# Attention weights of fifteen heads turned by a transposing DMA instead of TensorE

## The chip, the cores and the metric

The kernel runs on one core of one Trainium2 chip. The metric is the device time of one execution in microseconds; lower is better. Before the change the median of three runs is 2024.54 us (2023.59 to 2025.33).

## What is computed

One residual block on 512 rows of 2048 columns, in 32-bit floats: a norm, one input projection, sixteen attention heads of width 128 (eight with stick-breaking weights, eight with forgetting-gate softmax weights), a norm per head, an output projection, and a feed-forward part. The attention, cut to what matters here:

```python
# stick-breaking, per block of 128 queries:
z = einsum('bhqd,bhkd->bhqk', qb, kb) * scale
log_beta = log_sigmoid(z)
log_keep = where(causal, log_sigmoid(-z), 0.0)
rest = cumsum(log_keep, axis=3, reverse=True) - log_keep
a = where(causal, exp(log_beta + rest), 0.0)
o = einsum('bhqk,bhkd->bhqd', a, vb)
# forgetting: p = softmax(where(causal, z + c_q - c_k, -inf)); o = p @ vb
mixed = concat(head_rmsnorm(o_sb), head_rmsnorm(o_fox))
x = x + mixed @ w_out
```

## The kernel before

Every 32-bit matmul is done as three: each operand is split into a high part (ScalarE rounds it, `act.copy` to the type that TensorE reads in one pass) and a low part (VectorE subtracts the high part), and `mm3` (L74 to L78) multiplies high by high, high by low and low by high.

The attention stage runs in 17 periods, n = 0 to 16. In period n TensorE projects the q and k columns of head n (`project`: 16 row blocks of `w_in`, for q and then for k, three matmuls of 512 columns each, 96 in all, into the PSUM tile `accq`), computes the scores of head n - 1 (`scores`, into `s`), and forms the output of head n - 2 (`product`, into `o`) and the sums of squares of its norm (`norm_sums`, into `ssq`). Heads 0 to 7 in this order are forgetting heads, 8 to 15 stick-breaking heads. Period 16 has no projection left; it computes the last two heads' values (`accv`).

Between scores and product a head's weights pass through these steps. Stick-breaking: `start` and `soft` on ScalarE (absolute value, exponential, logarithm; L800, L803, L804), `maxed` on VectorE and a causal mask on GpSimd, `scan` (a running sum and a subtraction) on VectorE, `weights` on ScalarE (L817) and the mask again. Forgetting: `start` on VectorE with the mask, `maxed` on VectorE, `soft` on ScalarE, `scale` on VectorE. The result is `w`: 128 queries on the partitions by 1280 columns, the ten causal blocks of 128 by 128, in the places that `OFF_Q` gives.

The product needs the weights with the keys on the partitions. `turn` (L856 to L862) transposes the ten blocks on TensorE, against the identity, into the PSUM tile `pt`; `p_high` (ScalarE, L870) and `p_low` (VectorE, L873) split them into `ph` and `pl` in SBUF. `product` then multiplies, for each key block j, the value rows by the weights of queries j to 3 (512, 384, 256 and 128 columns, three matmuls each). `square`, `square_low`, `norm_sums`, `norm_1` (L914, L915) and `norm_2` (L920 to L923) make the head's norm; they reuse the buffers of `ph` and `pl`.

Beside that, ScalarE and VectorE split four 512 KB pieces of `w_in` per period (`wraw` to `wh` and `wl`, L168 and L175), scale and split q and k (`qf` to `uh` and `ul`), and form sums of `w_out` for the next stage (`WeightSums`: `tboth`, `thi`, `ws` or `mixed`), which SP stores to DRAM (`wraws`, `whigh`, `wsums`).

The order of every queue but GpSimd's comes from one list. `plan.at(t, f)` notes a job with a number, the place in the stage at which it should be issued; `Plan.run` sorts the jobs by it and calls them, and each engine, and SP with its DMAs, executes its own instructions in that order. The number sets nothing but the order. `TPER`, 27.05, is the number's step from period to period. Buffers and PSUM tiles have one copy each (`w`, `s`, `ph`, `pl`; `wraw` has three): a job waits until the last reader of what it overwrites is done.

Of the kernel before, what the change touches and what calls it, by code (L numbers as in the profile page):

```python
# [9 lines left out]
F32R = mybir.dt.float32r  # L10
AF = mybir.ActivationFunctionType
# [20 lines left out]
OFF_Q = [896, 1024, 512, 0]  # L32
# [4 lines left out]
def block_kernel(ctx, tc, x, g_attn, w_in, b_f, g_out_sb, g_out_fox, w_out, g_mlp, w_up, w_down, g_final, y):  # L37
# [667 lines left out]
    with tc.tile_pool(name="att", bufs=1, side="right", reuse_waits="tile") as at, \  # L705
# [69 lines left out]
        def causal(w, op, fill):  # L775

            for d, n in ((w[:, P:1280].rearrange("p (a b) -> p a b", b=384)[:, :, 256:], 3), (w[:, 896:1024], 1)):
                pool.affine_select(out=d, in_=d, compare_op=op, fill=fill, base=0,
                                   pattern=[[0, n], [-1, P]] if n > 1 else [[-1, P]], channel_multiplier=1)

        class Head:
# [4 lines left out]
            def scores(self):  # L786
                q, k = u_of[self.i, 0], u_of[self.i, 1]
                s = atp.tile([P, 1536], F32, tag="s", name="s")
                for i in (3, 2, 0, 1):
                    n = (i + 1) * P  # L790
                    qs = slice(i * P, (i + 1) * P)
                    mm3(s[:, OFF_Q[i]:OFF_Q[i] + n], q[0][:, qs], q[1][:, qs], k[0][:, :n], k[1][:, :n], i != 0, True)
                self.s = s[:, :1280]

            def plan_sb(self, plan, t):
                g = self.h

                def start():
                    self.w = wide("w")
                    act.activation(self.w, self.s, AF.Abs)  # L800

                def soft():
                    act.activation(self.w, self.w, AF.Exp, scale=-1.0)  # L803
                    act.activation(self.w, self.w, AF.Ln, bias=1.0)  # L804

                def maxed():
                    dve.scalar_tensor_tensor(self.w, self.s, 0.0, self.w, op0=ALU.max, op1=ALU.add)
                    causal(self.w, ALU.is_gt, 0.0)

                def scan():  # L810
                    for r in rows(self.w):

                        dve.tensor_tensor_scan(r[:, ::-1], r[:, ::-1], r[:, ::-1], 0.0, op0=ALU.add, op1=ALU.max)
                    dve.tensor_tensor(self.w, self.s, self.w, op=ALU.subtract)

                def weights():
                    act.activation(self.w, self.w, AF.Exp)  # L817
                    causal(self.w, ALU.is_gt, 0.0)

                for dt, f in ((8.45, start), (9.75, soft), (12.4, maxed), (15.2, scan), (20.1, weights)):  # L820
                    plan.at(t + dt, f)

            def plan_fox(self, plan, t):
# [28 lines left out]
                times = (6.5, 9.3, 11.0, 14.0) if self.i == 0 else (10.85, 14.6, 16.8, 20.1)  # L852
                for dt, f in zip((-4.0, *times), (load, start, maxed, soft, scale)):
                    plan.at(t + dt, f)
# [8 lines left out]

            def p_high(self):
                if self.i < 2 * NH - 1:
                    self.ph, self.pl = wide("ph", F32R), wide("pl", F32R)
                else:
                    both = at.tile([P, 2, 1280], F32R, tag="ws", name="p_last")
                    self.ph, self.pl = both[:, 0], both[:, 1]
                act.copy(self.ph, self.pt[:, :1280])  # L870
# [92 lines left out]
        def whole(m, t):  # L963
            w = WeightSums(m, (0, 1), lambda: mixed[:, :NH].rearrange("p (q a) n -> p q (a n)", a=2))
            loads, first, second = ((-15.0 if m > 1 else -13.5, 2.7), (21.5, 22.3, TPER + 3.3), (TPER + 1.75, TPER + 2.5, TPER + 6.7)) if m else \
                ((20.5, 20.6), (TPER + 1.75, TPER + 2.5, TPER + 4.5), (TPER + 10.0, TPER + 10.7, TPER + 7.0))
            for i in range(2):
                plan.at(t + loads[i], w.load, (i,))
            for i, at_ in enumerate((first, second)):
                for dt, f in zip(at_, (w.high, w.low, w.sum)):  # L970
                    plan.at(t + dt, f, i)
            third, fourth = (TPER + 9.2, TPER + 17.5) if m else (TPER + 7.2, 2 * TPER + 0.9)
            for dt, f in ((second[2] + 0.1, lambda: w.store(0, 2)), (third, lambda: w.sum(2)), (fourth, lambda: w.sum(3)),
                          (2 * TPER + 1.75, w.high_6), (2 * TPER + 2.5, w.low_6), (2 * TPER + 2.6, lambda: w.store(2, 4))):
                plan.at(t + dt, f)

        def half(m, d, n):
# [8 lines left out]
            jobs = [(17.6 if n == 8 else 8.3, load if n == 7 else w.load)]  # L986
            if d == 0:
                c, a = (23.2, (1.75, 2.4, 3.1, 3.8, 5.6, 6.4)) if n > 7 else (16.4, (5.5, 6.3, 7.0, 9.0, 12.0, 17.4))
                jobs += [(c, lambda: w.high(0)), (c + 0.7, lambda: w.low(0)), (c + 1.2, lambda: w.sum(0)), (c + 2.0 if n > 7 else TPER + 3.5, lambda: w.sum(1))]
                jobs += [(TPER + dt, f) for dt, f in zip(a, (lambda: w.high(1), lambda: w.low(1), lambda: w.sum(2), lambda: w.sum(3), w.high_6, w.low_6))]  # L990
                jobs += [(TPER + a[-1] + 0.1, w.store)]
            else:
                at_ = (23.7, 24.4, 25.1, TPER + 2.4) if n > 8 else [TPER + dt for dt in (2.4, 3.1, 6.4, 7.1)]
                jobs += [(dt, lambda j=j: w.sum(j)) for j, dt in enumerate(at_)] + [(at_[-1] + 0.1, w.store)]
# [19 lines left out]
        TRI, TPER = 0.681, 27.05  # L1014
# [4 lines left out]
        for n in range(2 * NH + 1):  # L1019
            t = TPER * n  # L1020
            i_s, i_o = n - 1, n - 2
            if n < 2 * NH:
                pieces = []
                for a, (which, hf) in enumerate(((0, 0), (0, 1), (1, 0), (1, 1))):
# [3 lines left out]
                    cast, low = ((-11.7, -6.9), (0.3, 5.4), (5.6, 10.9), (12.45, 13.95))[a]  # L1028
                    load = cast - 16 if n != 2 or a else -21.4
                    if n == 1:  # L1030
                        load = -23.0 if a == 0 else load
                        cast, low = ((-7.0, -5.0), (-3.0, -2.0), (2.9, 3.9), (8.5, 9.5))[a]
                    if n == 0:
                        cast, low, load = 16.3, 18.2, 0.3
                    pieces.append(q_piece(n, which, hf).plan(plan, t + load, t + cast, t + low))
                marks = [(0, 0, 1, 0.0), (0, 1, 6, 2.6), (0, 6, 8, 8.4), (1, 0, 8, 9.75), (2, 0, 8, 15.2), (3, 0, 4, 20.6), (3, 4, 8, 24.4)]
# [4 lines left out]
                for which, dt in ((0, {0: 19.0, 1: 25.85}.get(n, 21.4)), (1, TPER + 0.3)):  # L1041
                    plan.at(t + dt, scale_u, n, which)
                    plan.at(t + dt + (0.65 if (n, which) == (1, 0) else 0.75), high_u, n, which)
                    plan.at(t + dt + (1.35 if (n, which) == (1, 0) else 1.45), low_u, n, which)
            else:
                pieces = []
                for a in range(4):
# [3 lines left out]
                    cast, low = ((-11.7, -6.9), (0.3, 3.3), (9.0, 10.0), (13.0, 14.5))[a]  # L1051
                    pieces.append(w.plan(plan, t + cast - 16, t + cast, t + low))
                unit = 0
                for a in range(4):
                    for tt in range(TB):
                        dt = 1.45 * unit + (0 if unit < 2 else 1.95) + (0 if unit < 13 else 1.1)
# [4 lines left out]
            if 0 <= i_s < 2 * NH:  # L1061
                H = heads[i_s]
                ts = t + 6.45 if n < 2 * NH else t + 2.95
                plan.at(ts, H.scores)
                (H.plan_sb if H.h < NH else H.plan_fox)(plan, ts - 6.45)
                tp = t + (20.4 if n == 1 else 23.3) if n < 2 * NH else t + 2.9 + 1.95 + 1.45 * 11 - 0.05
                plan.at(tp, H.turn)
                plan.at(tp + 1.2, H.p_high)
                plan.at(tp + 2.5, H.p_low)
                if i_s % 2 == 0 and i_s < 2 * NH - 2:  # L1070
                    p_ = i_s // 2
                    plan.at(t - 12.0 if p_ else t + 3.0, load_v, p_)
                    plan.at(t + (5.4 if i_s >= NH else 16.5), high_v, p_)
                    plan.at(t + (6.3 if i_s >= NH else 23.65 if p_ else 17.0), low_v, p_)
            if 0 <= i_o < 2 * NH - 2:
                H = heads[i_o]
                plan.at(t + 0.68, H.product)
                plan.at(t + 2.7, H.square)
                plan.at(t + 4.6, H.square_low)
                plan.at(t + 6.0, H.norm_sums)  # L1080
                plan.at(t + 6.55, H.norm_1)
                plan.at(t + 7.95, H.norm_2)
# [981 lines left out]
```

## Time and profile before

| | |
|---|---|
| median of three runs | 2024.54 us |
| profiled execution: its own time | 2023.56 us |
| its span in the profile | 2021.8 us |
| granted TensorE clock | 0.999 of full speed |
| attention stage | about 168 to 583 us of the span |
| TensorE transposes of the weights | 160 (L861), ten for each of 16 heads |

In the views' lines stand: start and duration in us, engine, line of the kernel, operation, output and inputs by name (buffer numbers left out), shapes and count. An `[idle <-X]` at the end says how long the engine had been idle and who ended it. PE is TensorE's matmuls, PEld its weight loads, DVE VectorE, ACT ScalarE, POOL GpSimd, SP the engine that issues the DMAs. Matmuls overlap, so their cost is read from start to start, not from their duration. A line of the windows view gives a stretch, its length, each engine's busy time (and instructions), granted clock, DMA share and GB/s; one of the DMA view gives the count of transfers, the KB of each, and the median time from issue to landing; one of the waits view gives who waited for whom, us in total, how often, and the longest.

### The profile page before, as it was taken

The numbers are of one execution on the slowest core, as the hardware profiler recorded it, in microseconds if no ns is written. First come the engines' busy times: TensorE is split into PE (matmuls) and PEld (weight loads), VectorE is DVE, ScalarE is ACT, GpSimd is POOL, SyncE is SP. The second block draws the span as 40 slices with busy tenths as digits, with TensorE's granted clock in tenths as the row PEclk, the third lists the DMA queues.
The fourth block names the chain that finished last, engine by engine and source line by source line (L and its number), as shares of the span: only waits on it lengthen the run. The fifth ranks groups of instructions, "written<-read, shape, count | busy, mean of one in ns | idle before, by whom it ended". The sixth has DMA issues, their size and how long they took to land.

```text
span 2021.8 us, 27201 instructions
## 1 busy us (share of the span) xinstructions
PE 2012.6 (100%) x10421; PEld 1742.8 (86%) x10421; DVE 1739.4 (86%) x1971; ACT 1127.6 (56%) x1615; POOL 63.5 (3%) x72
## 2 busy tenths in 40 slices
PE   9999999999999999999999999999999999999998
PEld 9998888888898889888888888888888888888887
DVE  8876777888868579899999999998799888888896
ACT  7544444555555556676766767676644344443444
POOL 0000110000000000000000000000000000000004
PEclk9999999999999999999999999999999999999999
DMA  7418665665647982576666666666785674674642
GB/s 262 154 64 265 211 196 186 199 207 182 193 147 271 303 268 77 174 219 205 196 221 190 210 205 186 214 201 236 255 311 194 220 266 165 233 255 172 220 163 85
DMA packets 270195, 413.46 MB, mean 204 GB/s; under 512 B 10296, under 2 KB 165992, under 8 KB 263536
## 3 DMA queue, kind: packets, MB, share of 16 engines
q1 hardware_dynamic: 269312, 409.61, 61.1%
q10 hardware_dynamic: 752, 2.11, 0.3%
q8 instruction: 82, 1.34, 0.3%
q14 instruction: 49, 0.40, 0.1%
HBM read 315.19 MB, written 96.49 MB: 204 GB/s over the span
## 4 chain that ended last, share of the span: by engine, by line
PE 100%; ACT 0%; DVE 0%; issue 0%; ACTq 0%
PE psa L1236 11%; PE accd L77 8%; PE accd L76 8%; PE accd L78 8%; PE accq L76 6%; PE accq L78 6%; PE accq L77 6%; PE psa L1234 6%; PE psc L1236 5%; PE psc L1234 3%; PE psb L1236 3%; PE psb L1234 1%; PE m L76 1%; PE m L77 1%; PE m L78 1%; PE accoa L78 1%
## 5 line engine op out<-in xcount | busy, mean ns | idle before, releaser
L1872 ACT CAST wh<-wd 128x1024 fp32r<-128x1024 f32 x126 | 124.9, 999 | 168.9 <-PE accd L78 55.0
L1758 DVE TENSOR_TENSOR wl<-wu,wh 128x1024 fp32r<-128x1024 f32 x158 | 192.7, 1220 | 12.1 <-ACT wh L1752 12.0
L76 PE MATMUL accq<-hH,wh 128*128 128x512 f32 x512 | 201.4, 393 | 0.0
L78 PE MATMUL accq<-hH,wl 128*128 128x512 f32 x512 | 199.7, 390 | 0.0
L77 PE MATMUL accq<-hL,wh 128*128 128x512 f32 x512 | 199.6, 390 | 0.0
L1752 ACT CAST wh<-wu 128x1024 fp32r<-128x1024 f32 x158 | 167.5, 1060 | 44.1 <-issue 28.0
L1236 PE MATMUL psa<-f,wh 128*128 128x512 f32 x720 | 179.0, 391 | 0.0
L77 PE MATMUL accd<-wl,uf 128*128 128x512 f32 x436 | 169.6, 389 | 0.0
L78 PE MATMUL accd<-wh,uf 128*128 128x512 f32 x436 | 169.6, 389 | 0.0
L76 PE MATMUL accd<-wh,uf 128*128 128x512 f32 x436 | 169.4, 389 | 0.0
L1236 PEld LDWEIGHTS psa<-f,wh 128*128 128x128 f32 x720 | 132.3, 188 | 25.6
L1879 DVE TENSOR_TENSOR wl<-wd,wh 128x1024 fp32r<-128x1024 f32 x126 | 144.0, 1152 | 10.6 <-ACT wh L1872 10.6
L1593 DVE TENSOR_TENSOR m<-m,accd 128x1024 f32<-128x1024 f32 x84 | 102.3, 1217 | 46.1 <-PE accd L78 46.1
L1872 ACT CAST wx<-wd 128x1024 fp32r<-128x1024 f32 (+1 forms) x82 | 80.8, 995 | 106.9 <-PE accd L78 40.2
L78 PEld LDWEIGHTS accq<-hH,wl 128*128 128x128 f32 x512 | 96.1, 188 | 20.1
L77 PEld LDWEIGHTS accq<-hL,wh 128*128 128x128 f32 x512 | 96.2, 188 | 18.6
L76 PEld LDWEIGHTS accq<-hH,wh 128*128 128x128 f32 x512 | 96.3, 188 | 18.5
L76 PE MATMUL accd<-wx,uf 128*128 128x512 f32 x284 | 110.5, 389 | 0.0
L77 PE MATMUL accd<-wx,uf 128*128 128x512 f32 x284 | 110.5, 389 | 0.0
L78 PE MATMUL accd<-wx,uf 128*128 128x512 f32 x284 | 110.5, 389 | 0.0
L168 ACT CAST wh<-wraw 128x1024 fp32r<-128x1024 f32 (+1 forms) x70 | 72.7, 1040 | 60.8 <-PE accq L77 51.4
L1234 PEld LDWEIGHTS psa<-f,wl 128*128 128x128 f32 x720 | 96.0, 191 | 5.4
(444 smaller groups left out, 5087.6 us busy)
## 6 DMA issues: line engine op xcount, KB each, us to landing
wu<-in_w_up_dram SPq DMA_DIRECT2D x60, 1024.0 KB, 6.5
ufd<-st SPq DMA_DIRECT2D x98, 512.0 KB, 4.0
wd<-in_w_down_dram SPq DMA_DIRECT2D x48, 1024.0 KB, 8.0
uf<-ufd SPq DMA_DIRECT2D x42, 1024.0 KB, 7.3
wraw<-in_w_in_dram SPq DMA_DIRECT2D x68, 512.0 KB, 4.3
wo<-wsums SPq DMA_DIRECT2D x28, 512.0 KB, 4.7
q<-in_w_in_dram SPq DMA_DIRECT2D x32, 384.0 KB, 6.4
wd<-in_w_down_dram SPq DMA_DIRECT2D x16, 768.0 KB, 6.0
```

The source lines that it names most:

```text
L76: pe.matmul(out, sh, mh, start=first, stop=False, skip_group_check=True)
L77: pe.matmul(out, sh, ml, start=False, stop=False, skip_group_check=True)
L78: return pe.matmul(out, sl, mh, start=False, stop=last, skip_group_check=True)
L168: act.copy(self.hi, self.source())
L1234: ins = pe.matmul(ps[:, 2 * P:], lo[:, a, :], f_parts(p, a)[0], start=False, stop=last, skip_group_check=True)
L1236: ins = pe.matmul(ps, hi[:, a, :], f_both(p, a), start=a == PAIRS[0] and p in (1, 5), stop=last, skip_group_check=True)
L1593: dve.tensor_tensor(M[p][:, :, db, :], M[p][:, :, db, :], ps, op=ALU.add)
L1752: act.copy(rooms[k][0], srcs[k])
L1758: lows[0] = dve.tensor_tensor(lo, srcs.pop(k), hi.bitcast(F32), op=ALU.subtract)
L1872: act.copy(rooms[k + 3][0], srcs[k + 3])
L1879: dve.tensor_tensor(rooms[k + 2][1], srcs.pop(k + 2), rooms[k + 2][0].bitcast(F32), op=ALU.subtract)
```

## The change

For the first fifteen heads, `turn`, `p_high` and `p_low` are replaced by five steps:

- `halves`: ScalarE copies `w`, read as 2560 unsigned 16-bit elements, into `one`, with the 1280 low halves first and the 1280 high halves behind them;
- `turn_halves`: SP issues one transposing DMA from `one` to `two`, SBUF to SBUF, twenty blocks of 128 by 128 16-bit elements (640 KB);
- `join_halves`: ScalarE copies `two` to `pt`, now a buffer in SBUF, putting the two halves of each 32-bit element together again;
- `t_high` and `t_low`: the high copy on ScalarE and the subtraction on VectorE, from SBUF.

`one` and `pt` share a buffer, and `two` and `ph` share one (which `norm_2` of the head before still uses). Since the blocks stay in the order of `OFF_Q`, the product takes its columns block by block, in five groups. `OFF_Q` has new places, and the mask is applied to two blocks twice. The sixteenth head is turned on TensorE as before.

All periods are laid out anew: `TPER` becomes 26.05; the scores stand behind 24 of the period's projection matmuls; the join stands at 11.2 and the product at 16.5 of the period after the scores' (the product stood at 0.68, after a turn at 23.3); pieces of `w_in`, the splits and the sums of `w_out` have new places. The core of it:

```diff
-OFF_Q = [896, 1024, 512, 0]
+OFF_Q = [256, 0, 384, 768]
...
-            for d, n in ((w[:, P:1280].rearrange("p (a b) -> p a b", b=384)[:, :, 256:], 3), (w[:, 896:1024], 1)):
...
+            for d in (w[:, P:3 * P].rearrange("p (a b) -> p a b", b=P), w[:, 2 * P:].rearrange("p (a b) -> p a b", b=NT)[:, :, 3 * P:]):
+                pool.affine_select(out=d, in_=d, compare_op=op, fill=fill, base=0, pattern=[[0, 2], [-1, P]], channel_multiplier=1)
+
+        def apart(w):
+            return w.bitcast(U16).rearrange("p (h n) -> p h n", h=2)
+
+        def mingled(w):
+            return w.bitcast(U16).rearrange("p (n h) -> p h n", h=2)
...
+            def halves(self):
+                self.one = wide("pt")
+                act.copy(apart(self.one), mingled(self.w))
+
+            def turn_halves(self):
+                self.two = wide("ph")
+                sp.dma_start_transpose(self.two.bitcast(U16).rearrange("p (b t) -> p b t", t=P), self.one.bitcast(U16))
+
+            def join_halves(self):
+                self.pt = wide("pt")
+                act.copy(mingled(self.pt), apart(self.two))
+
+            def t_high(self):
+                self.ph, self.pl = wide("ph", F32R), wide("pl", F32R)
+                act.copy(self.ph, self.pt)
+
+            def t_low(self):
+                dve.tensor_tensor(self.pl, self.pt, self.ph.bitcast(F32), op=ALU.subtract)
...
+                    o, ph, pl = (w.rearrange("p (b t) -> p b t", t=P) for w in (self.o, self.ph, self.pl))
+                    for n, (j, to, of) in enumerate(((0, slice(0, 4, 2), slice(2, 4)), (0, slice(1, 4, 2), slice(0, 7, 6)),
+                                                     (1, slice(1, 4), slice(1, 8, 3)), (2, slice(2, 4), slice(5, 9, 3)),
+                                                     (3, slice(3, 4), slice(9, 10)))):
+                        last_heads[0] = mm3(o[:, to], v[0][:, j, hs], v[1][:, j, hs], ph[:, of], pl[:, of], n == 0, n == 4)
+                    return
...
-        TRI, TPER = 0.681, 27.05
+        TRI, TPER = 0.681, 26.05
...
+                if n < 2 * NH:
+                    plan.at(t + (25.2 if sb else 23.8), H.halves)
+                    plan.at(t + 26.2, H.turn_halves)
...
+                for dt, f in zip((11.25, 13.6, 19.3) if last_ else (11.2, 13.7, 14.9), (H.join_halves, H.t_high, H.t_low)):
+                    plan.at(t + dt, f)
...
+                plan.at(t + 16.5, H.product)
```

Where the order of instructions moves, three places matter. On TensorE, late in a stick-breaking period before the change, a head's ten transposes stand in one row between projection matmuls:

```order
L77 MATMUL accq<-hL_102,wh 128x512
L78 MATMUL accq<-hH_101,wl 128x512
L861 MATMUL pt<-ident,w 128x128 x10
L76 MATMUL accq<-hH_103,wh 128x512
L77 MATMUL accq<-hL_104,wh 128x512
```

After it that row is gone, and this is where the product of the head before begins, 63 projection matmuls and the scores into the period (lines are those of the changed file, one further down):

```order
L78 MATMUL accq<-hL_100,wh 128x512
L79 MATMUL accq<-hH_99,wl 128x512
L77 MATMUL o<-ph,vh 128x2x128
L78 MATMUL o<-pl,vh 128x2x128
L79 MATMUL o<-ph,vl 128x2x128
L77 MATMUL o<-ph,vh 128x2x128
L78 MATMUL o<-pl,vh 128x2x128
L79 MATMUL o<-ph,vl 128x2x128
L77 MATMUL o<-ph,vh 128x384
```

The product moved from the period's start to its middle, and its first group of 512 columns became two of 2 x 128. On ScalarE, behind the scores of a stick-breaking head, before the change:

```order
L800 ACTIVATE w<-s 128x1280
L803 ACTIVATE w<-w 128x1280
L804 ACTIVATE w<-w 128x1280
L168 CAST wh<-wraw 128x1024 x2
L817 ACTIVATE w<-w 128x1280
L742 CAST uh<-qf 128x512
L940 CAST tboth<-ws 128x512
L870 CAST ph<-pt 128x1280
```

And after it, in one of the three periods with a cast of `w_out` there:

```order
L806 ACTIVATE w<-s 128x1280
L809 ACTIVATE w<-w 128x1280
L810 ACTIVATE w<-w 128x1280
L968 CAST tboth<-ws 128x512
L880 COPY pt<-ph 128x2x1280
L884 CAST ph<-pt 128x1280
L169 CAST wh<-wraw 128x1024
L743 CAST uh<-qf 128x512
```

The join (L880) and the high copy (L884) of the head before now stand right behind the three activations of this head. On SP, among the DMAs of two stick-breaking periods after the change, the new instruction (L876) stands behind the load of a piece and ahead of the next ones:

```order
L964 DMA ws<-in_w_out_dram 128x2x512 x2
L162 DMA wraw<-in_w_in_dram 128x8x128
L876 DMA_TRANSPOSE ph<-pt 128x20x128
L162 DMA wraw<-in_w_in_dram 128x8x128 x2
L972 DMA wraws_92<-tboth 128x2x512
L162 DMA wraw<-in_w_in_dram 128x8x128
```

Nothing stood in its place before; all that is behind it on SP waits until it has been issued.

More of the change, by code (lines that the diff above doesn't have):

```diff
@@ L818, in weights @@
                     causal(self.w, ALU.is_gt, 0.0)
-                for dt, f in ((8.45, start), (9.75, soft), (12.4, maxed), (15.2, scan), (20.1, weights)):
+                last_ = self.i == 2 * NH - 1
+                for dt, f in zip((6.4, 7.7, 10.2, 14.5, 19.2) if last_ else (7.4, 8.7, 11.25, 16.45, 21.1), (start, soft, maxed, scan, weights)):
                     plan.at(t + dt, f)
@@ L850, in scale @@
                         dve.tensor_scalar(r, r, self.l[:, i:i + 1], None, op0=ALU.mult)
-                times = (6.5, 9.3, 11.0, 14.0) if self.i == 0 else (10.85, 14.6, 16.8, 20.1)
-                for dt, f in zip((-4.0, *times), (load, start, maxed, soft, scale)):
+                for dt, f in zip((-4.0, 7.4, 12.2, 15.5, 17.8), (load, start, maxed, soft, scale)):
                     plan.at(t + dt, f)
@@ L964, in whole @@
             w = WeightSums(m, (0, 1), lambda: mixed[:, :NH].rearrange("p (q a) n -> p q (a n)", a=2))
-            loads, first, second = ((-15.0 if m > 1 else -13.5, 2.7), (21.5, 22.3, TPER + 3.3), (TPER + 1.75, TPER + 2.5, TPER + 6.7)) if m else \
-                ((20.5, 20.6), (TPER + 1.75, TPER + 2.5, TPER + 4.5), (TPER + 10.0, TPER + 10.7, TPER + 7.0))
+            e, o = (t, t + TPER) if m else (TPER, TPER)
+            loads = (-4.0 if m == 1 else -15.0, 2.7) if m else (20.5, 20.6)
+            highs, lows_, sums_, sixth = ((e + 3.0, o + 3.0), (e + 4.75, o + 4.75), (e + 5.5, e + 16.4, o + 5.5, o + 16.4), (o + 10.2, o + 20.2)) if m else \
+                ((e + 4.3, e + 10.0), (e + 4.75, e + 10.9), (e + 5.5, e + 14.9, e + 19.6, e + 20.9), (e + 21.5, e + 23.3))
             for i in range(2):
                 plan.at(t + loads[i], w.load, (i,))
[L969 to L975, printed above, removed]
+                plan.at(highs[i], w.high, i)
+                plan.at(lows_[i], w.low, i)
+            for i in range(4):
+                plan.at(sums_[i], w.sum, i)
+            plan.at(sums_[1] + 0.1, lambda: w.store(0, 2))
+            plan.at(sixth[0], w.high_6)
+            plan.at(sixth[1], w.low_6)
+            plan.at(sixth[1] + 0.1, lambda: w.store(2, 4))
         def half(m, d, n):
@@ L1040, in block_kernel @@
                     plan.at(t + dt, project, n, (0, 0, 1, 1)[a], pieces[a], a % 2, k0, k1)
[L1041 to L1044, printed above, removed]
+                late = n <= NH
+                for which, times in ((0, (19.0, 19.75, 20.45) if n == 0 else (14.2, 14.95, 19.5) if late else (14.2, 16.0, 21.8)),
+                                     (1, (TPER + 0.3, TPER + 1.05, TPER + 2.6))):
+                    for dt, f in zip(times, (scale_u, high_u, low_u)):
+                        plan.at(t + dt, f, n, which)
             else:
@@ L1050, in block_kernel @@
                     w = Piece(w_in[k0 * P:(k0 + 4) * P, c:c + 2 * P].rearrange("(a p) c -> p a c", p=P), 4, 2 * P)
[L1051 to L1052 removed]
+                    cast, low = ((-11.15, -3.55), (2.0, 3.5), (3.7, 4.9), (10.25, 11.7))[a]
+                    pieces.append(w.plan(plan, t + (-21.0, -15.0, -14.0, -2.0)[a], t + cast, t + low))
                 unit = 0
```

78 lines of the change are left out of this document (40 added, 38 removed).

## The prediction

> **What bounds the kernel now.** I read the page first: busy shares, granted clock, the chain of work that ended last.
>
> ```profile
> span 2021.8 us, 27201 instructions
> PE 2012.6 (100%) x10421; PEld 1742.8 (86%) x10421; DVE 1739.4 (86%) x1971; ACT 1127.6 (56%) x1615; POOL 63.5 (3%) x72
> PEclk9999999999999999999999999999999999999999
> PE 100%; ACT 0%; DVE 0%; issue 0%; ACTq 0%
> ```
>
> TensorE (PE) is busy throughout, at full granted clock, and the chain is TensorE's alone. A busy PE can still hide waits, since matmul ends are modelled, so I next read start times in the attention stage (168 to 583 us). The timeline of PE around two heads' transposes:
>
> ```profile
> 414.64 0.39 PE L78 MATMUL accq<-hH,wl 128*128 128x512 f32 x1
> ...
> 416.00 0.39 PE L78 MATMUL accq<-hH,wl 128*128 128x512 f32 x1
> 416.23 1.25 PE L861 MATMUL pt<-ident,w 128*128 128x128 f32 x10
> 417.24 0.48 PE L76 MATMUL accq<-hH,wh 128*128 128x512 f32 x1
> 417.55 0.39 PE L77 MATMUL accq<-hL,wh 128*128 128x512 f32 x1
> ...
> 443.42 1.25 PE L861 MATMUL pt<-ident,w 128*128 128x128 f32 x10
> ```
>
> Six projection matmuls start in 416.00 - 414.64 us: 0.227 us each, though each "lasts" 0.39. A period is 443.42 - 416.23 = 27.19 us. From the start of the last matmul before the transposes to that of the second after them is 1.55 us; two matmuls would take 0.45, so ten transposes cost **1.10 us** of PE. The other engines over six periods, by the windows view (span, then PE, PEld, DVE, ACT, POOL):
>
> ```profile
> 416.23:579.35 163.12, 163.12 (x794) 138.08 (x792) 133.14 (x156) 92.56 (x107) 14.71 (x24) 1.00 0.57 176
> ```
>
> A period holds 22.2 us of VectorE (DVE) and 15.4 us of ScalarE (ACT). PE sets the period; DVE has 5 us to spare.
>
> **What the change takes from PE.** 150 transposes of 15 heads go: 15 x 1.10 = 16.5 us. The same product, weights per block as before, is issued in five groups of 256, 256, 384, 256 and 128 columns instead of four of 512, 384, 256, 128. The present product:
>
> ```profile
> 420.75 0.39 PE L76 MATMUL o<-ph,vh 128*128 128x512 f32 x1
> ...
> 421.43 0.33 PE L76 MATMUL o<-ph,vh 128*128 128x384 f32 x1
> ...
> 421.95 0.29 PE L76 MATMUL o<-ph,vh 128*128 128x256 f32 x1
> ...
> 422.32 0.22 PE L76 MATMUL o<-ph,vh 128*128 128x128 f32 x1
> ...
> 422.61 0.44 PE L76 MATMUL accq<-hH,wh 128*128 128x512 f32 x1
> ```
>
> It takes 1.86 us; the groups take 0.68, 0.52, 0.37 and 0.29. The new one takes 3 x 0.37 + 0.52 + 0.29 = 1.92, plus 0.06 a head, 0.9 us in all. Two of its groups read and write two separate 128-column blocks; no row shows that, but the blocks themselves are contiguous, so I count them like a plain group (bounds: nothing, and one more group start of about 0.1 us, 1.5 us in all). PE alone gives **-15.6 us**, and a period of 27.19 - 1.04 = 26.15 us.
>
> **What is added beside it.** Each head gets two ScalarE copies of 2560 16-bit elements and one transposing DMA; the high copy and the low subtraction stay, now read from SBUF. ScalarE's rows:
>
> ```profile
> 401.44 1.25 ACT L800 ACTIVATE w<-s 128x1280 f32<-128x1280 f32 x1 [0.54 <-PE s L78]
> 402.71 1.27 ACT L803 ACTIVATE w<-w 128x1280 f32<-128x1280 f32 x1
> 404.02 1.27 ACT L804 ACTIVATE w<-w 128x1280 f32<-128x1280 f32 x1
> 405.20 1.03 ACT L168 CAST wh<-wraw 128x1024 fp32r<-128x1024 f32 x1
> ...
> 417.52 1.23 ACT L870 CAST ph<-pt 128x1280 fp32r<-128x1280 f32 x1 [1.07 <-PE pt L861]
> ...
> 422.87 0.60 ACT L900 ACTIVATE ph<-o 128x512 f32<-128x512 f32 x1 [0.73 <-PE o L78]
> 423.36 0.58 ACT L901 COPY os<-o 128x512 f32<-128x512 f32 x1
> ```
>
> 1280 elements occupy it for 1.18 us (404.02 to 405.20), 512 for 0.49. So 2560 take about 2.4, and 2.5 if the next instruction needs the result. No row shows 16-bit elements with a 4-byte step: I bound them by 2.4 (one element a step, like every row here) and 4.8 (two steps each), and take 2.4. The load is then 15.4 + 4.8 = 20.2 of 26.15 us, and DVE stays at 22.2: neither becomes the bound by load. The two masks on GpSimd, now two blocks each, hold the same four blocks.
>
> **The new chain, by place in the order.** I count from a period's first projection matmul. PE: 24 matmuls to 5.45, scores 1.90 to 7.35 (the scores' first row starts at 399.34, the matmul behind them at 401.24), 24 matmuls to 12.80, 15 to 16.21, then the product, whose second matmul needs the low part at 16.34.
>
> ```profile
> 399.34 0.39 PE L76 MATMUL s<-uh 128*128 128x512 f32 x1
> ...
> 401.24 0.39 PE L76 MATMUL accq<-hH,wh 128*128 128x512 f32 x1
> ```
>
> Backwards from there: the low part takes 1.49 us and starts 1.26 after the high copy (417.52 to 418.78), and the join takes 2.5:
>
> ```profile
> 418.78 1.49 DVE L873 TENSOR_TENSOR pl<-pt,ph 128x1280 fp32r<-128x1280 f32 x1
> ```
>
> So the join must start by 16.3 - 1.49 - 1.26 - 2.5 = **11.0**. What can hold it back?
>
> *ScalarE itself.* In the seven periods with stick-breaking scores the join stands behind three activations that start 0.20 after the scores (7.55) and let the next instruction begin 405.20 - 401.44 = 3.76 later: 11.31. That is 0.3 late. In three of the seven a further cast of 512 (`tboth`) stands between: 0.8 late. 4 x 0.3 + 3 x 0.8 = **+3.6 us**, waits at the product that are new. In the seven forgetting-attention periods ScalarE is free before 11.0. There one job ahead of the join, `thi`, waits for a store, and today's waits view has it: 5.9 us in four waits. I take nothing for it (bounds 0 and 6).
>
> ```profile
> ACT thi L952 <- DMA wraws<-tboth: 5.9, 4, 4.0
> ```
>
> *The DMA.* It writes the buffer that the norm of the head before uses, and so starts after that norm's last step: today 430.29 + 0.75 - 426.72 = 4.3 us after L914, which follows the norm's matmuls. These now end near 22.7, so the DMA starts near 27.3, or 1.1 in the next period. Ahead of it on SP stands one 512 KB load, planned 2 us before the period's end and landing near 2.1.
>
> ```profile
> 426.72 0.69 ACT L914 ACTIVATE ra<-ssq,eps 128x512 f32<-128x512 f32 x1 [0.37 <-PE ssq L911]
> ...
> 430.29 0.75 DVE L923 SCALAR_TENSOR_TENSOR mixed<-os,g_rest,ph 128x512 f32<-128x512 f32 x1
> ```
>
> ```profile
> wraw<-in_w_in_dram SPq DMA_DIRECT2D x59, 512.0 KB, 4.1
> ...
> wraws<-tboth SPq DMA_DIRECT2D x15, 512.0 KB, 2.7
> ...
> whigh<-thi SPq DMA_DIRECT2D x8, 256.0 KB, 2.0
> ```
>
> No row shows a transposing DMA. It moves 640 KB. By the stores (2.0 us for 256 KB, 2.7 for 512) that is 3.1 us. The upper bound is by pieces: `wraw` moves 1024 runs of 512 B in 4.1 us, and 2560 runs of 256 B at that rate take 10.3. From 2.1 it lands between 5.2 and 12.4. The middle, 8.8, is before 11.0, so I count nothing, with 2 us to spare. Queued behind it on SP are loads of weight pieces cast 9 or more us after their issue place, against 4.1 us to land; they hide until the DMA holds SP's queue for some 5 us.
>
> [...]
>
> **The sum.** The profiled execution took 2023.56 us, 1.8 more than its span and 1.0 below the median of the three runs (2024.54). 2023.6 - 15.6 + 3.6 = 2011.6; I say **2012**.
>
> **The rivals.**
>
> *No new waits (2008).* If join and casts are a little quicker than the rows say, 3.6 us vanish: 2023.6 - 15.6. For it: the lateness is only 0.3 us in four of seven places. Against it: three places have 0.8.
>
> *A wait of about 1 us in every one of the 14 periods with a product (2022).* 14 us of the 15.6 are given back. For it: the chain join, high, low, product has no slack in any period, and each link crosses engines. Against it: DVE and ACT have 4 to 6 us free per period.
>
> *The DMA lands late (2028, slower from there).* The wait is then the landing minus 11.0 in seven periods and, beyond what is already counted, minus 11.3 in four and 11.8 in three: 14 L - 157.6. At L = 12.4, the bound by pieces, that is 16 us: 2028. From 12.4 on the change is slower than before by more than 4 us, and each further us costs 14. For it: 256 B runs are half as long as any large transfer's here. Against it: only the extreme bound reaches 12.4.
>
> *The 20 blocks of 128 x 128 are turned one after another.* At the landing time of the smallest transfer, 2.0 us, that is 40 us; L is 42.1 and the wait 14 x 42.1 - 157.6 = 432, some 2443 us. With SP's 0.37 us per issue it would be 7.4 us and hidden. For it: nothing in the trace, and 16 engines share every transfer here.
>
> [...]
>
> *16-bit elements at half speed on ScalarE (2028).* The join takes 2.4 us more, which the seven stick-breaking periods pay in full: 17 us. ScalarE would still fit, 25 of 26.15.
>
> *The transposes stay* is excluded: in the new order they are gone from 15 heads.
>
> **How the numbers follow.** Chances: forecast (2009 to 2016) 0.50; no waits 0.15; 1 us everywhere 0.10, of which 0.04 still counts as faster; DMA late 0.13, 0.02 of it within the same; half speed 0.07; blocks in series 0.05. A measurement of this kernel tells about 0.2%, 4 us, from no change: faster is below 2020.5, slower above 2028.6. Faster: 0.50 + 0.15 + 0.04 = 0.69; same: 0.06 + 0.02 = 0.08; slower 0.23. The range runs from 2007, no waits and 1 us of spread, to 2032; it leaves out the serial case, about half of the half-speed case and a third of the late DMA, some 0.17.
>
> **What would show it.** No L861 rows but ten; projection matmuls at 0.227 us; periods of 26.2 us with forgetting attention and 26.4 to 27.0 with stick-breaking. The gap between the first two `o` matmuls shows the wait at the product: 0.13 us if none. The join's row shows its releaser: the DMA if that is late, nothing if ScalarE is its own bound; its duration, 2.4 or 4.8, settles the 16-bit question. The DMA's landing belongs below 9 us after the issue. I am wrong if the join waits for the DMA in every period, if halves or join take over 3 us, or if PE waits elsewhere: scores late behind `ul`, a projection behind a piece's low part, or the norm's matmuls behind `square_low`.

## The result: 8.5 us slower

The changed kernel takes **2032.58 us** (median of four runs, 2030.32 to 2034.81) against 2024.07 us before, measured beside it (four runs, 2023.59 to 2025.33): ratio 1.0042, interval 1.0030 to 1.0054. The prediction was 2012. The profiled execution took 2030.32 us, 18.7 above the prediction's sum.

The page of the changed kernel: span, busy shares, and the chain that ended last.

```profile
span 2028.6 us, 27079 instructions
PE 2004.1 (99%) x10316; PEld 1733.7 (85%) x10316; DVE 1740.5 (86%) x1971; ACT 1204.0 (59%) x1645; POOL 60.3 (3%) x72
...
PE 79%; ACT 4%; DVE 3%; DMA 3%; issue 1%; ACTq 0%; SPq 0%; DVEq 0%
```

Before, the chain was TensorE's alone (100%). Now it passes through ScalarE, VectorE and a DMA: somewhere TensorE stands and waits for them. The first thing to check is the new work itself. The rows of the tile `pt` (minimum, median and maximum in ns, then first and last start) and the landing of the transposing DMA (minimum, median, maximum from issue):

```profile
L872 ACT COPY pt<-w x15: 2310/2310/2321, 198.8 to 587.5; 128x2560 uint16<-128x2560 uint16 x15
...
L880 ACT COPY pt<-ph x15: 3087/3105/3161, 212.6 to 602.3; 128x2560 uint16<-128x2560 uint16 x15
```

```profile
L876 SPq DMA_TRANSPOSE ph<-pt x15: 2417/2566/8168, 202.4 to 590.7; - x15
...
DMA to landing us min/median/max: 4.1/4.2/10.2
```

The halves cost what was taken for them (2.31 against 2.4). The join does not: 3.10 against 2.4 to 2.5. The DMA lands 4.2 us after its issue; the prediction allowed it 9. Next, who waits for whom in the attention stage (us in total, times, longest):

```profile
ACT thi L980 <- DMA wraws<-tboth: 13.5, 4, 4.3
PE o L78 <- DVE pl L887: 10.2, 11, 1.1
...
ACT tboth L968 <- DMA wraws<-tboth: 8.8, 4, 4.3
...
PE o L77 <- ACT ph L884: 4.7, 3, 2.0
...
ACT pt L880 <- DMA ph<-pt: 3.1, 3, 1.3
```

The join (L880) hardly waits for its DMA, 3.1 us in three places. It waits in periods 2, 4 and 6 only, and the product loses nothing by it in 4 and 6 and 0.3 us in 2. What is large is `thi` and `tboth` on ScalarE: these are casts of `w_out`, into a buffer that the store of the cast before still reads. Seven of these waits stand right ahead of a join, `thi` in periods 3, 5 and 7 and `tboth` in 8, 10, 12 and 14. And TensorE waits for the low and the high part at the product (`o`).

The periods come from the starts of the transposing DMA: before, each lasted 27.19 us; after, the 13 from 229.77 us (period 3) on last, in order, 27.11, 26.10, 27.17, 26.09, 27.35, 27.08, 27.21, 29.58, 27.21, 30.27, 27.21, 31.31 and 27.28. Two without a wait take 26.1, as TensorE's own sum said (26.15). The 13 together take 360.97 us, against 353.5 before and 339.3 at 26.1: **21.7 us of waits and slow clock where 14.2 were saved**. Eight periods lose about 1.1 us each (8.8); three, the even ones with stick-breaking scores (10, 12 and 14), lose 3.5, 4.2 and 5.2 (12.9). The eight are of two kinds: in 9, 11, 13 and 15, the odd ones with stick-breaking scores, nothing that waits stands ahead of the join; in 3, 5, 7 and 8 a cast does.

An odd stick-breaking period, 11, in the timeline:

```profile
453.85 1.24 ACT L806 ACTIVATE w<-s 128x1280 f32<-128x1280 f32 x1 [1.13 <-PE s L79]
...
456.44 1.27 ACT L810 ACTIVATE w<-w 128x1280 f32<-128x1280 f32 x1
457.62 3.10 ACT L880 COPY pt<-ph 128x2560 uint16<-128x2560 uint16 x1
460.75 1.26 ACT L884 CAST ph<-pt 128x1280 fp32r<-128x1280 f32 x1
462.05 1.49 DVE L887 TENSOR_TENSOR pl<-pt,ph 128x1280 fp32r<-128x1280 f32 x1 [0.75 <-ACT ph L884]
462.46 0.28 PE L77 MATMUL o<-ph,vh 128*128 128x256 f32 x1
463.60 0.39 PE L78 MATMUL o<-pl,vh 128*128 128x256 f32 x1 [0.86 <-DVE pl L887]
```

Scores, three activations, join, high, low, product: each starts when the one before ends, and TensorE, on time at 462.46, starts its second matmul 1.14 us later. The same place in an even stick-breaking period, 10:

```profile
426.86 1.28 ACT L810 ACTIVATE w<-w 128x1280 f32<-128x1280 f32 x1
429.90 0.62 ACT L968 CAST tboth<-ws 128x512 fp32r<-128x512 f32 x1 [1.76 <-DMA wraws<-tboth]
430.43 3.09 ACT L880 COPY pt<-ph 128x2560 uint16<-128x2560 uint16 x1
...
432.66 0.39 PE L79 MATMUL accq<-hH,wl 128*128 128x512 f32 x1
433.55 1.26 ACT L884 CAST ph<-pt 128x1280 fp32r<-128x1280 f32 x1
434.86 0.39 PE L77 MATMUL o<-ph,vh 128*128 128x256 f32 x1 [1.81 <-ACT ph L884]
...
436.38 0.39 PE L78 MATMUL o<-pl,vh 128*128 128x256 f32 x1 [1.14 <-DVE pl L887]
```

ScalarE stands still for 1.76 us in front of the cast, with the join behind it; the join's DMA was issued at 417.88 and, by the median of 4.2 us, had landed some 8 us earlier. TensorE now waits twice. Period 8, the last with forgetting scores, has such a cast too, and this one waits longer, but from an earlier time, so that the join is less late:

```profile
373.08 0.62 ACT L968 CAST tboth<-ws 128x512 fp32r<-128x512 f32 x1 [4.29 <-DMA wraws<-tboth]
```

Why the store of period 10 landed so late is in SP's own rows:

```profile
417.88 2.63 SPq L876 DMA_TRANSPOSE ph<-pt  x1
421.29 1.50 SPq L162 DMA_DIRECT2D wraw<-in_w_in_dram  x2
423.03 0.75 SPq L972 DMA_DIRECT2D wraws<-tboth  x1
```

The store was issued at 423.03, as soon as its low part was done; two loads of 512 KB had gone out 1.7 and 0.6 us ahead of it. The cast that needs its buffer starts at 429.90, 6.9 us after the issue (the profile lacks this store's own landing; in period 12, with the same two loads ahead, it is 5.9 us). Over the stage the stores' median is 4.7 us, before it was 2.7:

```profile
wraws<-tboth SPq DMA_DIRECT2D x15, 512.0 KB, 4.7
...
ph<-pt SPq DMA_TRANSPOSE x14, 4.2
```

Taken one by one, the stores from 200 us on fall into groups by what SP issued just ahead of them:

| loads issued ahead of the store | kernel before | changed kernel | the experiments below |
|---|---|---|---|
| none in the last 2 us | 2.7 | 2.7 to 4.1 | 2.7 to 4.2 |
| one, 1.2 us ahead | 3.9, 4.1 | | |
| one, 0.6 us ahead | 5.1 | 5.4 to 5.7 | 5.2 to 5.6, once 6.8 |
| two, 1.7 and 0.6 us ahead | | 5.9 | 6.1 to 6.9 |

The figures are us from the store's issue to its landing, where the profile has it. In the kernel before, which has no transposing DMA, a store was nearly as late when a load stood 0.6 us ahead of it.

Here the description of the kernel before has to be corrected. It says that SP, too, issues in the order of the list. `free_loads` takes SP out of that order early in the stage; from then on a scheduler places its DMAs. The list has one of these loads at 11.05, behind the store; on the chip both stand ahead of it.

### The profile page after: what moved, and what is told of

Same layout as the page of the kernel before. It is cut to its first block, busy times and chain, and to the rows that moved or that the text cites. A ratio compares the mean times of both kernels' runs of the same rounds, so it can differ in the third digit from the quotient of the medians.

```text
span 2028.6 us, 27079 instructions
## 1 busy us (share of the span) xinstructions
PE 2004.1 (99%) x10316; PEld 1733.7 (85%) x10316; DVE 1740.5 (86%) x1971; ACT 1204.0 (59%) x1645; POOL 60.3 (3%) x72
## 4 chain that ended last, share of the span: by engine, by line
PE 79%; ACT 4%; DVE 3%; DMA 3%; issue 1%; ACTq 0%; SPq 0%; DVEq 0%
PE psa L1280 11%; PE accd L79 8%; PE accd L78 8%; PE accd L77 8%; PE psa L1278 6%; PE psc L1280 5%; PE psc L1278 3%; PE psb L1280 3%; PE accq L77 2%; PE accq L78 2%; PE accq L79 2%; DMA wraws<-tboth 2%; ACT pt L880 2%; PE psb L1278 1%; PE m L78 1%; PE m L79 1%
## 5 line engine op out<-in xcount | busy, mean ns | idle before, releaser
L1278 PE MATMUL psa<-f,wl 128*128 128x256 f32 x720 | 98.3, 283 | 0.0
```

The lines of the kernel that those rows point to most:

```text
L1278: ins = pe.matmul(ps[:, 2 * P:], lo[:, a, :], f_parts(p, a)[0], start=False, stop=last, skip_group_check=True)
```

## The experiments

Three theories. **A**: the join is late, because it takes 3.1 us and because the casts ahead of it on ScalarE wait for stores; the chain join, high, low, product has no slack. **B**: the transposing DMA costs the time itself, by landing late, by holding SP or by slowing the other transfers. **C**: the engines are short of time under the added copies. Four kernels ran on one chip beside the kernel before (2024.09 us there), four on another (2024.08); for the changed kernel the time above stands.

### Own buffers for the second cast

The second `tboth` cast of the heads of the even periods goes to two buffers of its own, so that it needs no store to have landed (its own store then goes out as two DMAs of 256 KB). What is added:

```diff
 def high(self, i):
+    if i == 1 and self.own is not None:
+        self.two_ = self.own.bitcast(F32R), at.tile([P, NT], F32R, tag="ul5", name="tlow")
+        act.copy(self.two_[0], self.q[2][:, :NT])
+        return
...
```

> The second cast of the w_out sums gets buffers of its own in the three stick-breaking periods that have it ahead of the join, so that it no longer waits for the store of the first (1.8, 0.9 and 1.9 us in the changed kernel's trace); its 0.5 us on ScalarE stays. Theory A (the join is late because casts ahead of it wait for stores, and because it takes 3.1 us instead of 2.4): these three periods fall from 29.6, 30.3 and 31.3 us to about 27.7, the slow clock behind the longest waits goes too, and the time falls by 5 to 8 us to about 2023 to 2026. Theory B (the transposing DMA itself is what is late or slows all else): the three periods and the time stay as they are.

Measured 2022.72 us (2021.74 to 2023.70), ratio 0.9993 (0.9984 to 1.0002): level with the kernel before, and 10 us below the changed one. The even periods fall from 29.6, 30.3 and 31.3 to 27.80, 27.84 and 27.84. ScalarE at the place shown above:

```profile
427.31 1.27 ACT L810 ACTIVATE w<-w 128x1280 f32<-128x1280 f32 x1
428.49 0.60 ACT L971 CAST ws<-ws 128x512 fp32r<-128x512 f32 x1
429.00 3.11 ACT L880 COPY pt<-ph 128x2560 uint16<-128x2560 uint16 x1
```

No idle time is left ahead of the cast, and the join stands 0.5 us behind it, as the order alone would have it. The transposing DMA is untouched. A holds; B would have left these periods long.

### The join written in order

Each 32-bit element's two halves are now written next to each other and read from two places, 2560 bytes apart; the same copy in another order.

```diff
-act.copy(mingled(self.pt), apart(self.two))
+act.copy(self.pt.bitcast(U16).rearrange("p (n h) -> p n h", h=2), self.two.bitcast(U16).rearrange("p (h n) -> p n h", h=2))
```

> The join writes its 2560 elements in the order of memory and takes them in turn from the two halves, so that the write has no 4-byte step and the read alternates. Theory A: the extra 0.8 us of the join (3.10 against 2.31 for the parting copy, same count) comes from the write with a step; the join falls to about 2.3, each of 14 product waits shrinks by up to 0.8, and the time falls by 8 to 11 us to about 2020. If the price is that of 16-bit pairs from two places, the join stays at 3.1 or grows, and the time with it. Theory B: no change whatever the join takes.

Measured 2025.68 us (2023.56 to 2027.09), ratio 1.0006 (0.9996 to 1.0015). The join, among the rows of `pt`:

```profile
L880 ACT COPY pt<-ph x15: 2621/2643/2655, 212.8 to 597.2; 128x2560 uint16<-128x2560 uint16 x15
```

It takes 2.64 us, not the 2.3 expected, so the new order takes away 0.46 of the 0.8 us that the join takes over the halves. The edit changes the order of the write and that of the read together; what each is worth alone was not tried. The time is above the 2020 that was expected, as the join gave less than it should. Each odd stick-breaking period is shorter by what the join saves, 26.75 instead of 27.21. So the join's length goes straight to the end, as A says.

### A plain copy instead of the transposing DMA

The weights are copied and not transposed, so the product multiplies the wrong blocks; all else stands.

```diff
-sp.dma_start_transpose(self.two.bitcast(U16).rearrange("p (b t) -> p b t", t=P), self.one.bitcast(U16))
+sp.dma_start(self.two.bitcast(U16), self.one.bitcast(U16))
```

> The transposing DMA is replaced by a plain DMA of the same 640 KB from the same to the same buffer; the weights are left untransposed. Theory A: the DMA was in time already (landing 4.2 us after issue, the join waited 3.1 us for it in all), so little changes: within 4 us of the changed kernel, the product waits the same. Theory B: transposing is what costs; stores land again after 2.7 us, the waits behind them go, and the time falls by 8 us or more.

Measured 2031.96 us (2029.71 to 2034.43), ratio 1.0038 (1.0025 to 1.0051): the time of the changed kernel. The DMA view of the stage:

```profile
ph<-pt SPq DMA_DIRECT2D x15, 640.0 KB, 3.2
wraws<-tboth SPq DMA_DIRECT2D x15, 512.0 KB, 5.3
```

The copy lands 1.0 us sooner than the transposing DMA, and nobody is better off: the stores land no sooner (5.3 us), and the stick-breaking periods last 27.2 (odd) and 30.8 to 30.9 us (even). Its issue held SP for 0.5 us, where the transposing one held it for 2.4 us or more. So neither the transposing nor its hold on SP costs the time. What 640 KB more for each head, moved either way, do to the other transfers this kernel can't tell.

### Turned twice

The transposing DMA is issued twice, the second over the first.

```diff
-sp.dma_start_transpose(self.two.bitcast(U16).rearrange("p (b t) -> p b t", t=P), self.one.bitcast(U16))
+for _ in range(2):
+    sp.dma_start_transpose(self.two.bitcast(U16).rearrange("p (b t) -> p b t", t=P), self.one.bitcast(U16))
```

> Each head's transposing DMA is issued twice in a row to the same place, the second after the first. It would land about 8.5 us after the first issue, some 10 us into the period. Theory A: the join, which starts near 11.3 in stick-breaking periods, still finds it landed there; stores behind it land later, so that casts ahead of the join wait up to 4 us longer in seven periods: 0 to 25 us slower. Theory B, where the DMA decides: 14 times 4 us, 50 us slower or more.

Measured 2080.67 us (2079.12 to 2082.35), ratio 1.0281 (1.0264 to 1.0298): 48 us more than the changed kernel. That is outside the 0 to 25 us expected by A, and next to the 50 of B: issued twice, the DMA does cost the time. Now the join does wait for its data, 31.8 us in seven places:

```profile
ACT pt L881 <- DMA ph<-pt: 31.8, 7, 10.1
```

Each period lasts 30 to 31 us, and the mean granted clock falls from 0.998 to 0.986, which over 2077 us is 25 us by estimate, about half of the 48; the expectation had left the clock out. This does not bring B back for the changed kernel, where the single DMA is hardly waited for. But its slack is less than what one more such transfer takes, about 4 us: that it lands in time is a matter of a few us.

### The sixth sum's cast later

In the forgetting periods 3, 5 and 7 the cast `thi` stands ahead of the join and waits for a store. It moves behind the join.

```diff
-(o + 10.2, o + 20.2)) if m else \
+(o + 17.6, o + 20.2)) if m else \
```

> The cast thi of the w_out sums is moved from ahead of the join to behind the softmax exponentials in the three odd forgetting periods 3, 5 and 7; all else is the changed kernel. Theory A (a cast that waits some 4 us for a store holds the join): the product waits of 0.9 to 1.2 us in these periods go, they fall from about 27.1 to 26.1 us like their neighbours, and the time falls by 3 us to about 2029.5. Theory C (these periods are longer because they hold more VectorE and ScalarE work): they stay at 27.1.

Measured 2029.98 us (2027.56 to 2031.46), ratio 1.0027 (1.0016 to 1.0038). ScalarE ahead of a join in period 5, in the changed kernel:

```profile
287.36 1.05 ACT L169 CAST wh<-wraw 128x1024 fp32r<-128x1024 f32 x1
292.51 0.62 ACT L980 CAST thi<-mixed 128x512 fp32r<-128x512 f32 x1 [4.11 <-DMA wraws<-tboth]
293.04 3.10 ACT L880 COPY pt<-ph 128x2560 uint16<-128x2560 uint16 x1
```

The join starts 10.1 us after the issue of its transposing DMA (282.98). With the edit it starts 5.3 us after it (286.92 behind 281.59), and the product's first two matmuls follow each other:

```profile
296.53 0.28 PE L77 MATMUL o<-ph,vh 128*128 128x256 f32 x1
296.64 0.28 PE L78 MATMUL o<-pl,vh 128*128 128x256 f32 x1
```

The three periods fall from 27.11, 27.17 and 27.35 to between 26.09 and 26.10, that is to no wait. The join came 4.7 us sooner and the period gained about 1 us, so the join had some 3.6 us to spare there. The median time fell by 2.6 us, as expected, but the spreads of the two kernels overlap, and in the profiled execution the even stick-breaking periods were 3.5 us longer in all than in that of the changed kernel. The finding rests on the periods.

### High and low parts in two slices

`t_high` and `t_low` are each split in two instructions of 640 columns, so that the low part starts behind the first half of the high part and the product behind the first half of the low one.

```diff
-act.copy(self.ph, self.pt)
+for c in (slice(0, 640), slice(640, 1280)):
+    act.copy(self.ph[:, c], self.pt[:, c])
...
-dve.tensor_tensor(self.pl, self.pt, self.ph.bitcast(F32), op=ALU.subtract)
+for c in (slice(0, 640), slice(640, 1280)):
+    dve.tensor_tensor(self.pl[:, c], self.pt[:, c], self.ph[:, c].bitcast(F32), op=ALU.subtract)
```

> The high copy and the low subtraction of the turned weights are each done in two halves of 640 columns, so that VectorE begins after half of the copy and TensorE after half of the subtraction. Theory A (in the periods without a waiting cast the product waits for the plain length of the chain join, high, low): of each wait some 0.6 to 0.7 us goes, the odd stick-breaking periods fall from 27.2 to about 26.5, and the time falls by 8 to 10 us to about 2023. Theory C (the engines are short of time in the period): no gain, or a loss by four more instructions a period.

Measured 2020.57 us (2018.00 to 2022.88), ratio 0.9982 (0.9972 to 0.9991): 12 us below the changed kernel, with join, casts, stores and DMA all as they were. An odd stick-breaking period, here 9, now lasts 26.4 to 26.5 us (one 26.9), where it lasted 27.2; the even ones still 28.7 to 30.0:

```profile
388.45 2.94 SPq L876 DMA_TRANSPOSE ph<-pt  x1
414.84 2.63 SPq L876 DMA_TRANSPOSE ph<-pt  x1
```

Periods 3, 5, 7 and 8, with their casts waiting as before, fall to 26.1 to 26.3. Shortening the chain moved the end here, as the shorter join did (6.9 us). By C, one more instruction on ScalarE and on VectorE for each head (two in all, not the four that the expectation counts) should have cost time; it gained time.

### Own buffers, and the cast earlier

The first experiment's edit, with the second cast and its subtraction moved ahead of the scores' activations as well.

```diff
-a = ... (4.85, 6.2, 8.3, 9.0, 9.7, 11.15, 12.75, 13.45, 16.6, 23.2)
+a = ... (4.85, 6.2, 8.3, 9.0, 9.7, 4.9, 9.8, 13.45, 16.6, 23.2)
```

> As the kernel with buffers of its own for the second cast, with that cast and its subtraction also moved ahead of the scores' activations, where ScalarE and VectorE stand idle for about 1 us. Theory A: the remaining 0.5 us ahead of the join goes too; the three even stick-breaking periods fall from 27.8 to about 27.2 like the odd ones, and the time from 2022.7 to about 2021.

Measured 2020.25 us (2019.76 to 2022.24), ratio 0.9981 (0.9972 to 0.9991). The join of the even period starts right behind the activations:

```profile
428.18 3.10 ACT L880 COPY pt<-ph 128x2560 uint16<-128x2560 uint16 x1
```

Even stick-breaking periods last 27.28 us, as do the odd ones, 27.15 to 27.25: the 0.5 us by which the even ones fell from 27.8 was the cast's own time.

### All four together

Own buffers with the cast early, the sixth sum's cast later, the join in order, high and low in two.

> All four mends together: second cast in its own buffers and early, thi later, join written in order, high and low in two halves. Theory A: the product waits are gone but for one in period 8, periods are 26.1 to 26.4 us, and the time is what TensorE's own sum gives, 15 us below the kernel before: about 2010. Theory C (14 us a period of added work is too much for these engines): above 2016, with waits at other places.

Measured **2008.93 us** (2008.73 to 2009.16, four runs), ratio 0.9925 (0.9911 to 0.9940): 15.1 us below the kernel before, 23.7 below the changed one. On SP, two transposing DMAs a period apart, and at the product of that period the first two matmuls:

```profile
439.27 3.00 SPq L876 DMA_TRANSPOSE ph<-pt  x1
...
465.30 2.46 SPq L876 DMA_TRANSPOSE ph<-pt  x1
```

```profile
454.21 0.28 PE L77 MATMUL o<-ph,vh 128*128 128x256 f32 x1
454.32 0.28 PE L78 MATMUL o<-pl,vh 128*128 128x256 f32 x1
```

This period is 26.03 us, the even ones beside it last 26.16, and no product waits but that of period 2, by 0.2 us. 15.1 of TensorE's 15.6 us came out once the join's chain was in time, with one more instruction on ScalarE and on VectorE for each head than in the changed kernel and the transposing DMA in place. That settles A against B and C.

## Why the prediction was wrong, step by step

*What PE saves: right.* 15.6 us predicted; 15.1 in the last experiment, and 26.10 us in the changed kernel's undisturbed periods against 26.15. That the groups of two separate blocks cost no more than plain ones is within this. (In the paragraph on chances, what the range leaves out adds up to 0.13 by its own terms, 0.05, half of 0.07 and a third of 0.13, and not to 0.17.)

*The DMA: right.* Predicted to land 5.2 to 12.4 us into the period, middle 8.8, in time for a join at 11. It took 4.2 us from its issue (median), so that in the stick-breaking periods it landed some 5.3 to 6.1 us into the period, by an estimate from the product's start, near the lower bound and some 3 us before the middle. The join waited for it in three places, 3.1 us in all. The rivals "DMA lands late" and "blocks in series" did not happen: twenty blocks took 4.2 us together. An ordinary DMA of the same 640 KB landed in 3.2 us, 1.0 sooner.

*The load of the engines: right.* ScalarE was busy 123.8 of 172.9 us in the stick-breaking part, VectorE 132.9, and neither was the bound; nor did the last experiment, with more instructions on both, show any such bound.

*The size of the join: wrong.* "I bound them by 2.4 and 4.8, and take 2.4": halves and join were given one price. The halves read with a step and write in one run: 2.31. The join writes with a step: 3.10, inside the bounds but 0.7 above the value, and over the 3 us that the prediction itself named as a sign of being wrong. The four odd stick-breaking periods were to be 0.3 us late and were 1.1 to 1.2 late. A price inside the bounds mattered because the chain had no slack; the rival "a wait of about 1 us in every one of the 14 periods" named that, at 0.10, and four periods (9, 11, 13 and 15) came out so. That 3, 5, 7 and 8 lost about as much is a coincidence: there a waiting cast ate the join's slack first.

*The casts ahead of the join: the step that failed most.* This is the term +3.6 us of the sum, and the nothing counted beside it for the forgetting periods. For the three even stick-breaking periods the prediction counted the cast `tboth` as 0.5 us of ScalarE's time. It did not ask what the cast itself waits for: the store of the cast before, from the same buffer. For `thi` it did ask, quoted 5.9 us in four waits, and took nothing. The `tboth` ahead of the join in period 8 it overlooked: "ScalarE is free before 11.0" did not hold there. All these waits turn on how long a store takes to land, and the prediction used the 2.7 us of the profile before; with a load issued 0.6 us ahead it was 5.4 to 5.7, and with two the cast of the even period shown could start only 6.9 us after the issue. At 2.7 the store would have landed at 425.7, before ScalarE came to the cast at 428.1. The three even periods, the join's own lateness and the clock among it, lost 12.9 us against 2.4 predicted, and the periods 3, 5, 7 and 8 lost 1.0 to 1.25 each, 4.3 in all, against nothing.

*The sum.* 21.7 us of waits and slow clock in 13 periods against 3.6 predicted is 18.1 of the 18.7 us by which the profiled execution misses the sum. About 3 of them are not waits at all, but the clock, which the prediction did not foresee (below).

What stays open: that the loads ahead make the stores late is read from the stores' landings in all these kernels, the one before included; a kernel with another order on SP alone was not tried. The experiments show what the waits for the stores cost, whatever made the stores late.

## What to carry to other kernels

When work moves from the engine that bounds the kernel to a chain across three others, count the slack of that chain, not the load of its engines: here ScalarE was idle for over a quarter of the stick-breaking part, and the chain through it still cost 21.7 us, slow clock included. For each instruction that stands ahead of the chain on one of its engines, ask what it waits for, a store's landing above all (in period 10 ScalarE stood still for 1.76 us in front of such a cast, with the join behind it), and whether the new neighbours on that queue change this landing (a median of 2.7 us before, 4.7 after). Splitting the chain's steps in slices, so that the next step starts on the first one, was worth as much (12 us) as taking the waiting casts of the three even periods out of the way.

## What was not expected of the hardware

*The granted clock fell behind two short waits on TensorE, to 0.64 and 0.79 in period 12, and in other periods it did not.* The windows view of the changed kernel, three us each (busy time and instructions of PE, PEld, DVE, ACT and POOL, then the granted clock), around the product of period 12, whose first two matmuls waited 0.92 and 1.14 us:

```profile
489.00:492.00 3.00, 1.22 (x5) 0.56 (x3) 1.26 (x1) 2.97 (x4) 0.00 (x0) 1.00 0.12 46
492.00:495.00 3.00, 2.72 (x13) 2.72 (x14) 3.00 (x5) 0.70 (x2) 0.00 (x0) 0.64 0.25 89
495.00:498.00 3.00, 3.00 (x12) 2.49 (x13) 2.51 (x4) 2.54 (x4) 0.00 (x0) 0.79 0.01 4
498.00:501.00 3.00, 3.00 (x15) 2.48 (x14) 2.33 (x3) 0.69 (x2) 2.30 (x2) 1.00 0.13 17
```

TensorE was idle for 0.92 and 1.14 us; behind that the clock is 0.64 and 0.79 for six us. The matmuls of this stretch show it too, in PE's timeline:

```profile
495.23 0.73 PE L77 MATMUL accq<-hH,wh 128*128 128x512 f32 x1
495.76 0.62 PE L78 MATMUL accq<-hL,wh 128*128 128x512 f32 x1
496.19 0.43 PE L79 MATMUL accq<-hH,wl 128*128 128x512 f32 x1
496.45 0.39 PE L77 MATMUL accq<-hH,wh 128*128 128x512 f32 x1
```

They start 0.53, 0.43 and 0.26 us apart, where 0.227 is usual. The same stands behind the product of period 14, which waited 1.98 and 1.14 us (clock 0.81 and 0.62 from 549 to 555 us), but not in period 10, which waited 1.81 and 1.14 (clock 1.00 from 436 to 442). In the kernel with high and low parts in two slices, waits of 1.01 and 0.47 us in period 14 had it (from 545.93 us the `accq` matmuls start 0.53, 0.43 and 0.43 us apart), and 1.40 and 0.48 in period 10 did not (clock 1.00 from 432 to 441). The kernel before, the two with own buffers and no other edit, and the last one, in all of which no product waits more than 1.14 us, show no such stretch in the attention stage (mean granted clock 0.999 in each). By an estimate from the two windows, 3 x 0.36 + 3 x 0.21, a stretch costs up to 1.7 us beyond the wait. What decides whether the slow clock follows a wait, no run here shows: its length alone does not, as 1.01 and 0.47 us had it and 1.40 and 0.48 did not.

*A copy on ScalarE that writes 16-bit elements in steps of 4 bytes was slower than those that write them in one run*: 2560 elements in 3.10 us, against 2.31 when they are written in one run and read in steps, and 2.64 when written in one run from two places by turns.
